# The opening of a two-layer mixer backbone in another order

## The chip, the cores and the metric

The kernel runs on one NeuronCore of a Trainium2 chip. The metric is device time in microseconds (us) for one launch. Five engines work beside each other: TensorE (PE in the profile; PEld is its weight loads), VectorE (DVE), ScalarE (ACT), GpSimd (POOL) and SyncE (SP, which here only issues transfers). Each runs its own instructions in the order in which the program gave them to it.

## The reference

Two layers over 256 latent tokens `x` and 256 context tokens `ctx`, width 1024, all in fp32.

```python
x = x + pos_embed_2d(rows)                      # before layer 0
for l in range(DEPTH):                          # DEPTH = 2
    mod = c_act @ w_mod[l] + b_mod[l]           # c_act = silu(c); ctx the same with c_ctx
    sh1, sc1, ga1, sh2, sc2, ga2 = split(mod, 6)
    h = rms_norm(x, g_norm1[l]) * (1 + sc1) + sh1
    z = h @ w_in[l]                             # 1024 x 5376
    states = s5_states(z[..., :256], discretise(lam, log_dt, b), ctx_final)
    x = x + ga1 * token_mixer(z, states, p)     # S5 readout, Fourier, pooling, convolution, gates, w_out
    x = x + ga2 * sq_relu_mlp(modulate(x, g_norm2[l], sh2, sc2), w1[l], w2[l])
return rms_norm(x, g_final)
```

`discretise` makes the recurrence's coefficients from the parameters: exponentials, a sine and a cosine, a quotient.

## The kernel before

All activations lie transposed in SBUF: `X[:, k, :]` is 128 channels by 512 tokens (context, then latent), k from 0 to 7. A product in fp32 accuracy is made of three matmuls of rounded halves: every operand is split into a high part (ScalarE, a copy into fp32r) and a low part (VectorE, a subtraction). In the profile the halves lie in tiles called `parts`, PSUM in `bank`, the recurrence's data in `scan`, X and scratch in `whole`, and most of the mixers' scratch in `mixer`. All engines' calls go through one wrapper, so that nearly every row says L64, and rows are told apart by tile and shape. Weights come as 128x1024 blocks through `Stream`: three raw slots, from which ScalarE makes the high and VectorE the low halves.

The change is in the opening, that is `run` and the first part of `layer(0)`. Its parts are these.

- **Loads.** SP's queue brings x in four blocks (`whole<-in_x_dram`), the modulation weights in 16 blocks (`in_w_mod_dram`), the first input weights (`in_w_in_dram`) and the recurrence's parameters (`in_s5p_dram`). ScalarE's queue brings the position tables, the conditioning and constants.
- **Sums of squares.** For each k the position is added to the latent half, ScalarE squares the tile, and the eight squares are added up. TensorE then sums over the partitions (four matmuls 128x1), and `norm_steps` takes the inverse root by ten small steps on VectorE. Four products of the result with the identity (`d`) and four matmuls with ones spread it to all partitions (`r`).
- **Modulation.** `parts(n)` runs n steps of `mod_part`: each is eight small matmuls (128x128 blocks, output 32x128) with one weight block. The fourth step of a set ends with a ScalarE copy of the sums (`MODSB`). `mod_finish(m)` then issues one matmul 128x8 with a selection matrix, and an addition and a scaled product on VectorE, which give shift and scale for tiles m and m+1 of h.
- **h and its products.** `next(h)` makes one tile of h: high halves on ScalarE (two ACTIVATE 128x256), the low half on VectorE and ScalarE; VectorE multiplies the next tile of X by `r`. `group(k, j)` is the product of h tile k with weight block j, three matmuls 128x512: the first needs only high halves, the second the low half of h. Four weight blocks have a PSUM bank each, into which the eight tiles of h are added. `weight(j)` has the halves of block j made.
- **Fill.** `warm(n)` issues n matmuls 128x256 whose result is not read.
- **Preparation.** `S5.prep` is a generator of small VectorE operations on 128x16 tiles (`scan<-scan`) that makes the recurrence's coefficients; `step(tab[0], n)` runs it up to its n-th next yield. When it is done, two tasks start that build tables from the coefficients, one on GpSimd and one on VectorE. They are interleaved with the mixers of layer 0 by a planner that keeps an estimated clock.

After the opening the remaining 38 blocks of the input projection, the recurrence and the other mixers follow, then projections and the MLP.

## Time and profile before

| | us |
|---|---|
| median of 3 runs | 1206.25 (1205.58 to 1209.96) |
| the profiled execution | 1209.18 |
| its span, first to last instruction | 1207.2 |
| TensorE busy | 1160.9 (96%) |
| VectorE busy | 976.1 (81%) |
| GpSimd busy | 282.9 (23%) |

The span is what the trace shows; 2 us of the profiled execution's time lie outside it. A share is an average over the span. TensorE's idle time, 46.3 us in all, lies in few places, and each of them has an engine or a transfer that it waited for.

### The profile page before, as it was taken

Reading aid. Unit: us, or ns where it says so; the run is one execution under the profiler, and the core shown is the slowest. Engines: PE = TensorE matmul, PEld = TensorE weight load, DVE = VectorE, ACT = ScalarE, POOL = GpSimd, SP = SyncE. Lnnn points to the kernel's source line nnn. Section 1 sums busy time; section 2 is a strip of 40 time slices with the busy share of each in tenths; the row PEclk is TensorE's granted clock in tenths of the full one; section 3 lists DMA queues with packets and bytes.
Section 4 is the critical chain, followed back from the end, with each engine's and each line's share of the span. In section 5 each row is a group of like instructions: output and inputs, shape, how many; then the busy total and the mean of one; then the engine's idle time right before and its main releaser. Section 6 shows DMA issues by size and latency. Waiting matters only on the chain.

```text
span 1207.2 us, 20297 instructions
## 1 busy us (share of the span) xinstructions
PE 1160.9 (96%) x7770; PEld 1009.4 (84%) x7770; DVE 976.1 (81%) x1878; ACT 517.1 (43%) x872; POOL 282.9 (23%) x319
## 2 busy tenths in 40 slices
PE   7999897999999999999999899999899999999997
PEld 5777675777888988888887778898899999999997
DVE  6789989977999769999988883546998788867764
ACT  4534242344324365422332333346544556645543
POOL 0038656000000100166555561020520001000000
PEclk9999999999999999999999999999899999999999
DMA  9543531644674514466578774425554545555551
GB/s 366 225 144 109 180 92 52 229 156 138 212 229 156 173 37 148 140 188 230 186 245 296 249 247 180 130 98 177 173 166 167 159 160 205 177 190 179 189 182 48
DMA packets 66513, 211.49 MB, mean 175 GB/s; under 512 B 7984, under 2 KB 13616, under 8 KB 66416
## 3 DMA queue, kind: packets, MB, share of 16 engines
q1 hardware_dynamic: 55456, 183.84, 45.4%
q10 hardware_dynamic: 7696, 14.56, 3.3%
q0 software_dynamic: 3264, 11.80, 2.9%
q8 instruction: 61, 1.00, 0.3%
q14 instruction: 36, 0.29, 0.1%
HBM read 199.19 MB, written 10.98 MB: 174 GB/s over the span
## 4 chain that ended last, share of the span: by engine, by line
PE 72%; DVE 15%; POOL 3%; DMA 3%; issue 3%; ACT 3%; ACTq 0%; POOLq 0%; DVEq 0%; SPq 0%
PE bank L64 72%; DVE scan L64 5%; DVE parts L64 4%; DVE mixer L64 2%; DVE whole L64 2%; ACT parts L64 2%; POOL tables L64 1%; POOL whole L64 1%; ACT whole L64 1%; DVE windows L64 1%; POOL scan L64 1%; DMA whole<-in_w_in_dram 1%; DMA whole<-in_x_dram 0%; DMA scan<-scr_z 0%; DMA scr_c<-tables 0%
## 5 line engine op out<-in xcount | busy, mean ns | idle before, releaser
L64 PE MATMUL bank<-parts 128*128 128x512 f32 (+2 forms) x4008 | 727.2, 339 | 19.0 <-DVE parts L64 16.6
L64 PEld LDWEIGHTS bank<-parts 128*128 128x128 f32 x4008 | 616.3, 191 | 105.4 <-DVE parts L64 22.3
L64 ACT ACTIVATE parts<-whole 128x1024 fp32r<-128x1024 f32 (+1 forms) x288 | 273.7, 959 | 144.9 <-PE bank L64 73.9
L64 DVE TENSOR_TENSOR parts<-whole,parts 128x1024 fp32r<-128x1024 f32 (+1 forms) x240 | 294.0, 1233 | 16.0 <-ACT parts L64 15.6
L64 PE MATMUL bank<-hidden,parts 128*128 128x256 f32 (+1 forms) x1440 | 251.2, 335 | 0.0
L64 PEld LDWEIGHTS bank<-hidden,parts 128*128 128x128 f32 x1440 | 217.5, 188 | 29.9 <-issue 0.3
L64 DVE SCALAR_TENSOR_TENSOR whole<-whole 128x1024 f32<-128x1024 f32 (+4 forms) x188 | 175.7, 936 | 15.2 <-DMA whole<-in_w_modt_dram 12.0
L64 POOL TENSOR_TENSOR whole<-whole 128x256 f32<-128x256 f32 (+1 forms) x69 | 50.3, 743 | 347.2 <-ACT whole L64 342.2
L64 DVE SCALAR_TENSOR_TENSOR whole<-bank,whole 128x256 f32<-128x256 f32 (+1 forms) x121 | 54.7, 475 | 66.4 <-PE bank L64 66.2
L64 ACT ACTIVATE whole<-whole 128x256 f32<-128x256 f32 (+2 forms) x139 | 48.9, 388 | 107.2 <-DVE whole L64 96.4
L64 ACT ACTIVATE mixer<-bank 128x512 f32<-128x512 f32 (+1 forms) x84 | 40.7, 496 | 119.8 <-PE bank L64 110.3
L64 DVE TENSOR_TENSOR whole<-whole 128x256 f32<-128x256 f32 (+7 forms) x158 | 73.0, 467 | 16.7 <-ACT whole L64 11.7
L64 ACT ACTIVATE whole<-bank 128x512 f32<-128x512 f32 (+2 forms) x69 | 35.5, 537 | 109.1 <-PE bank L64 77.5
L64 POOL TENSOR_TENSOR tables<-tables,whole 128x256 f32<-128x256 f32 x48 | 61.4, 1287 | 37.4 <-DMA scr_c<-tables 34.9
L64 DVE TENSOR_TENSOR hidden<-whole,hidden 128x512 fp32r<-128x512 f32 (+2 forms) x77 | 53.4, 698 | 9.0 <-ACT hidden L64 2.4
L64 ACT ACTIVATE hidden<-whole 128x512 fp32r<-128x512 f32 (+2 forms) x77 | 47.1, 615 | 8.2 <-PE bank L64 2.3
L64 ACT ACTIVATE tables<-bank 128x512 f32<-128x512 f32 (+2 forms) x20 | 8.4, 422 | 92.8 <-PE bank L64 92.5
L64 POOL COPY whole<-whole 128x32 f32<-128x32 f32 x20 | 11.9, 626 | 150.3 <-DVE whole L64 150.3
L64 POOL TENSOR_TENSOR scan<-scan,whole 128x256 f32<-128x256 f32 (+3 forms) x50 | 44.0, 892 | 12.0 <-DVE scan L64 8.3
L64 DVE SCALAR_TENSOR_TENSOR scan<-scan,whole 128x512 f32<-128x512 f32 (+1 forms) x64 | 42.7, 728 | 0.0
L64 PE MATMUL bank<-merged,parts 128*128 128x256 f32 (+1 forms) x240 | 38.0, 316 | 0.8 <-DVE merged L64 0.8
L64 DVE TENSOR_TENSOR scan<-scan,whole 128x256 f32<-128x256 f32 (+5 forms) x61 | 31.5, 543 | 9.0 <-ACT whole L64 8.0
(115 smaller groups left out, 899.0 us busy)
## 6 DMA issues: line engine op xcount, KB each, us to landing
whole<-in_w_dram SPq DMA_DIRECT2D x128, 512.0 KB, 4.3
whole<-in_w_in_dram SPq DMA_DIRECT2D x84, 512.0 KB, 4.3
whole<-in_w_modt_dram SPq DMA_DIRECT2D x78, 512.0 KB, 4.1
whole<-in_w_br_dram SPq DMA_DIRECT2D x16, 512.0 KB, 4.4
whole<-in_w_out_dram SPq DMA_DIRECT2D x16, 512.0 KB, 4.2
mixer<-in_w_mod_dram SPq DMA_DIRECT2D x8, 512.0 KB, 9.7
scan<-scr_b POOLq DMA_DIRECT2D x8, 512.0 KB, 5.2
scan<-in_w_mod_dram SPq DMA_DIRECT2D x6, 512.0 KB, 9.7
```

Of the source, the lines that this page charges most:

```text
L64: return f(out, *a, **k)
```

## The change

The parameters' first 48 columns are loaded ahead of x, and `prep` is stepped from the start: a `yield` is added between its two loads, and 17 of its steps lie in the opening, where it was 10. The two position loads become one, issued first. All position additions run on VectorE, where GpSimd had three of the eight. Squares are added in pairs (four additions in place of seven), and TensorE sums each pair over the partitions as it comes, into one bank, four matmuls a pair. The fill matmuls ahead of this are 3, with 1 after each of the first two pairs, where it was 7. Loads of modulation and input weights alternate in another order, and the modulation steps and products of h are interleaved one by one. `d` is made ahead of `mod_finish(0)`.

```diff
         K.nc.sync.dma_start(par, K.I["s5p"][self.l][:, 0:48])
+        yield
         K.nc.sync.dma_start(raw, K.I["s5p"][self.l][:, 48:560])
...
-    def norm_steps(self, accs, n, width, d=None):
+    def norm_steps(self, accs, n, width, d=None, pss=None):
-        pss = [self.aux() for _ in accs]
+        pss = pss or [self.aux() for _ in accs]
...
 
+            prep = tab[0]
             parts(2)
-            self.warm(2)
-            norm = self.norm_steps(((self.ACC,),), 512, 1024)
+            norm = self.norm_steps((), 512, 1024, pss=[self.sums])
             next(norm)
             self.warm(2)
             parts(1)
-            self.warm(0)
+            self.warm(1)
+            y = [y for y in norm][-1]
             parts(1)
-            y = [y for y in norm][-1]
-            self.warm(1)
+            d = self.tmp()
+            for i in range(4):
+                nc.vector.tensor_scalar(d[:, 128 * i:128 * i + 128], self.ident, y[:, i:i + 1], None, op0=MUL)
             self.mod_finish(0)
-            self.warm(2)
-            d, r = self.tmp(), self.aux()
+            r = self.aux()
             for i in range(4):
                 sl = slice(128 * i, 128 * i + 128)
-                nc.vector.tensor_scalar(d[:, sl], self.ident, y[:, i:i + 1], None, op0=MUL)
                 nc.tensor.matmul(r[:, sl], self.ones, d[:, sl], start=True, stop=True)
-            self.warm(4)
+            self.warm(2)
             h = self.h_tiles(l, 0, r, 0, 512)
+            next(h)
             weight(0)
             next(h)
+            group(0, 0)
             next(h)
-            group(0, 0)
-            self.stream.advance(1)
+            self.step(prep, 1)
             self.mod_ahead = 16
             parts(1)
-            next(h)
+            group(1, 0)
+            parts(1)
             weight(1)
+            self.step(prep, 2)
+            group(0, 1)
             parts(1)
-            group(1, 0)
-            weight(2)
-            parts(2)
-            group(0, 1)
+            group(1, 1)
+            parts(1)
             self.mod_finish(2)
             next(h)
             next(h)
-            group(1, 1)
+            self.step(prep, 1)
+            group(2, 0, 1)
+            parts(1)
+            weight(2)
+            group(3, 0, 1)
+            parts(1)
+            self.step(prep, 3)
             group(0, 2)
             group(1, 2)
-            self.step(tab[0], 3)
-            group(2, 0, 1, 2)
             parts(1)
+            group(2, 2)
             weight(3)
-            group(3, 0)
             parts(1)
-            group(3, 1)
-            parts(1)
-            parts(1)
-            group(3, 2)
             self.mod_finish(4)
             next(h)
             next(h)
+            self.step(prep, 1)
+            group(3, 2)
             group(0, 3)
             group(1, 3)
+            parts(1)
+            group(4, 0, 1, 2)
+            parts(1)
+            group(5, 0, 1, 2)
+            parts(1)
             group(2, 3)
             group(3, 3)
-            self.step(tab[0], 3)
-            group(4, 0, 1)
-            parts(2)
-            group(4, 2)
-            parts(2)
-            group(4, 3)
+            parts(1)
             self.mod_finish(6)
+            self.step(prep, 2)
             next(h)
             next(h)
-            self.step(tab[0], 3)
-            group(5, 0, 1, 2, 3)
+            group(4, 3)
+            group(5, 3)
+            self.step(prep, 2)
             group(6, 0, 1, 2, 3)
             group(7, 0, 1, 2, 3)
         else:
...
-        prow, pcol = self.SCRA(16), self.SCRA(256)
+        pos = self.SCRA(272)
+        nc.scalar.dma_start(pos, I["pos"])
-        nc.scalar.dma_start(prow, I["pos"][:, 0:16])
-        nc.scalar.dma_start(pcol, I["pos"][:, 16:272])
-        for k in range(0, 8, 2):
-            nc.sync.dma_start(self.X[:, k:k + 2, :], I["x"][:, k:k + 2, :])
...
 
         self.tab0.append(self.start(make0(), "d", 0.0))
-        self.mod_load()
-        while self.stream.load():
-            pass
-        self.step(self.tab0[0], 1)
-        self.mod_ahead = 8
+        prep = self.tab0[0]
+        self.step(prep, 1)
+        for k in range(0, 8, 2):
+            nc.sync.dma_start(self.X[:, k:k + 2, :], I["x"][:, k:k + 2, :])
+        for ahead in (3, 4, 8):
+            self.mod_ahead = ahead
+            self.mod_load()
+            self.stream.load()
+            if ahead == 4:
+                self.step(prep, 1)
+        self.mod_ahead = 10
         self.mod_load()
         nc.vector.memset(self.CACT, 0.0)
-        self.warm(7)
+        self.step(prep, 2)
         t = self.tmp()
         nc.scalar.activation(t[:, 0:16], cc, AF.Sigmoid)
         nc.vector.tensor_tensor(self.CACT[:, :, 0:2], t[:, 0:16].rearrange("p (k c) -> p k c", c=2),
                                 cc.rearrange("p (k c) -> p k c", c=2), op=MUL)
-        pr = prow.rearrange("p (k r) -> p k r", k=4)
-        pc = pcol.rearrange("p (k r) -> p k r", k=4)
+        pr = pos[:, 0:16].rearrange("p (k r) -> p k r", k=4)
+        pc = pos[:, 16:272].rearrange("p (k r) -> p k r", k=4)
+        self.warm(3)
+        self.sums = self.aux()
         sq = []
         for k in range(8):
             x = self.X[:, k, 256:512].rearrange("p (r c) -> p r c", r=4)
             pe = bc(pr[:, k, :, None], [128, 4, 64]) if k < 4 else bc(pc[:, k - 4, None, :], [128, 4, 64])
-            (nc.gpsimd if k in (1, 3, 5) else nc.vector).tensor_tensor(x, x, pe, op=ADD)
+            nc.vector.tensor_tensor(x, x, pe, op=ADD)
             sq.append(self.ACC if k == 0 else self.SIGR[k % 4] if k < 5 else self.TMP[k % 4])
             nc.scalar.activation(sq[k], self.X[:, k, :], AF.Square)
-            if k in (3, 4):
-                nc.vector.tensor_tensor(sq[k - 3], sq[k - 3], sq[k - 1], op=ADD)
-        V = nc.vector.tensor_tensor
-        for i, j in ((1, 5), (0, 4), (0, 1), (0, 6), (0, 7)):
-            V(sq[i], sq[i], sq[j], op=ADD)
+            if k % 2:
+                nc.vector.tensor_tensor(sq[k - 1], sq[k - 1], sq[k], op=ADD)
+                for i in range(4):
+                    nc.tensor.matmul(self.sums[:, i:i + 1], sq[k - 1][:, 128 * i:128 * i + 128], self.ones[:, 0:1],
+                                     start=k == 1 and i == 0, stop=k == 7 and i == 3)
+                if k < 5:
+                    self.warm(1)
+        self.step(prep, 1)
```

The first place is the start of TensorE's program, up to the spreading of the norm. `bank_63` with 128x256 is fill, 128x1 are sums of squares, 32x128 are modulation steps. Before:

```order
L64 MATMUL bank_63<-whole 128x256 x7
L64 MATMUL bank_70<-whole 32x128 x8
L64 MATMUL bank_70<-mixer,whole 32x128 x8
L64 MATMUL bank_63<-whole 128x256 x2
L64 MATMUL bank_68<-whole 128x1 x4
L64 MATMUL bank_63<-whole 128x256 x2
L64 MATMUL bank_70<-mixer,whole 32x128 x16
L64 MATMUL bank_63<-whole 128x256
L64 MATMUL bank_69<-whole 128x8
L64 MATMUL bank_63<-whole 128x256 x2
L64 MATMUL bank_67<-whole 128x128 x4
L64 MATMUL bank_63<-whole 128x256 x4
```

And now:

```order
L64 MATMUL bank_63<-whole 128x256 x3
L64 MATMUL bank_68<-whole 128x1 x4
L64 MATMUL bank_63<-whole 128x256
L64 MATMUL bank_68<-whole,mixer 128x1 x4
L64 MATMUL bank_63<-whole 128x256
L64 MATMUL bank_68<-whole,mixer 128x1 x4
L64 MATMUL bank_68<-whole 128x1 x4
L64 MATMUL bank_70<-whole 32x128 x8
L64 MATMUL bank_70<-mixer,whole 32x128 x8
L64 MATMUL bank_63<-whole 128x256 x2
L64 MATMUL bank_70<-mixer,whole 32x128 x8
L64 MATMUL bank_63<-whole 128x256
```

The sums stand ahead of all modulation steps, in four sets, and the fill ahead of them has become shorter.

The second place is TensorE around `mod_finish(2)`, whose matmul is `bank_68<-whole 128x8`; `parts` 128x512 are products of h. Before, from the first product's end:

```order
L64 MATMUL bank_70<-mixer,whole 32x128 x8
L64 MATMUL bank_70<-scan,whole 32x128 x8
L64 MATMUL bank_64<-parts 128x512 x3
L64 MATMUL bank_70<-scan,whole 32x128 x16
L64 MATMUL bank_65<-parts 128x512 x3
L64 MATMUL bank_68<-whole 128x8
L64 MATMUL bank_65<-parts 128x512 x3
L64 MATMUL bank_66<-parts 128x512 x6
L64 MATMUL bank_64<-parts 128x512 x3
L64 MATMUL bank_65<-parts 128x512 x3
L64 MATMUL bank_66<-parts 128x512 x3
```

And now, from the sixth modulation step:

```order
L64 MATMUL bank_70<-scan,whole 32x128 x8
L64 MATMUL bank_65<-parts 128x512 x3
L64 MATMUL bank_70<-scan,whole 32x128 x8
L64 MATMUL bank_65<-parts 128x512 x3
L64 MATMUL bank_70<-scan,whole 32x128 x8
L64 MATMUL bank_68<-whole 128x8
L64 MATMUL bank_64<-parts 128x512 x3
L64 MATMUL bank_65<-parts 128x512 x3
L64 MATMUL bank_70<-scan,whole 32x128 x8
L64 MATMUL bank_64<-parts 128x512 x3
```

Before, nine matmuls of h tiles 0 and 1 stand between that matmul and the first of tile 2. Now the last modulation step stands directly ahead of it, and products of tile 2 directly behind it.

The third place is VectorE around `mod_finish(6)`, whose two operations are `128x2x4` and `128x4`; `scan` 128x16 is preparation, `parts` rows are low halves of h and weights. Before, the finish is followed by h tile 6:

```order
L64 TENSOR_TENSOR whole<-bank_68,whole 128x2x4
L64 SCALAR_TENSOR_TENSOR whole<-whole 128x4
L64 TENSOR_SCALAR whole<-whole 128x256
L64 TENSOR_TENSOR whole<-whole,bank_67 128x512
L64 TENSOR_TENSOR parts<-whole,parts 128x256
L64 SCALAR_TENSOR_TENSOR parts<-whole 128x256
L64 TENSOR_SCALAR whole<-whole 128x256
L64 TENSOR_TENSOR parts<-whole,parts 128x256
L64 SCALAR_TENSOR_TENSOR parts<-whole 128x256
```

And now:

```order
L64 TENSOR_TENSOR whole<-bank_68,whole 128x2x4
L64 SCALAR_TENSOR_TENSOR whole<-whole 128x4
L64 TENSOR_SCALAR scan<-scan 128x16 x2
L64 SCALAR_TENSOR_TENSOR scan<-scan 128x16
L64 TENSOR_TENSOR scan<-scan 128x16 x2
L64 TENSOR_SCALAR scan<-scan 128x16 x2
L64 SCALAR_TENSOR_TENSOR scan<-scan 128x16
L64 TENSOR_SCALAR whole<-whole 128x256
L64 TENSOR_TENSOR whole<-whole,bank_67 128x512
L64 TENSOR_TENSOR parts<-whole,parts 128x256
L64 SCALAR_TENSOR_TENSOR parts<-whole 128x256
L64 TENSOR_SCALAR whole<-whole 128x256
```

Eight preparation operations have come between the finish and h tile 6.

## Rows read from the trace of the kernel before

**Rows 1.** Head of the page: span, and TensorE's busy time.
```profile
span 1207.2 us, 20297 instructions
...
PE 1160.9 (96%) x7770; PEld 1009.4 (84%) x7770; DVE 976.1 (81%) x1878; ACT 517.1 (43%) x872; POOL 282.9 (23%) x319
```
**Rows 2.** Waits of TensorE over the whole span: total, times, longest.
```profile
PE bank L64 <- DVE parts L64: 16.6, 10, 7.8
...
PE bank L64 <- POOL scan L64: 3.9, 2, 2.1
```
**Rows 3.** Windows by stage: length, each engine's busy time, granted clock, DMA share, GB/s.
```profile
77.40:211.40 134.00, 118.33 (x707) 92.06 (x705) 126.94 (x219) 48.23 (x121) 92.27 (x112) 0.95 0.32 107
211.40:427.00 215.60, 214.95 (x1304) 176.00 (x1304) 182.81 (x302) 80.17 (x113) 9.43 (x12) 0.99 0.54 181
```
**Rows 4.** Timeline of TensorE in the opening: start, time, instructions, idle before.
```profile
4.47 6.32 PE L64 MATMUL bank<-whole 128*128 128x256 f32 x14 [4.47 <-DMA whole<-in_x_dram]
...
17.59 4.44 PE L64 MATMUL bank<-whole 128*128 128x256 f32 x24
22.54 0.50 PE L64 MATMUL bank<-parts 128*128 128x512 f32 x1 [0.51 <-ACT parts L64]
23.60 0.73 PE L64 MATMUL bank<-parts 128*128 128x512 f32 x2 [0.56 <-DVE parts L64]
...
26.07 0.73 PE L64 MATMUL bank<-parts 128*128 128x512 f32 x2 [0.29 <-DVE parts L64]
26.74 1.08 PE L64 MATMUL bank<-scan,whole 128*32 128x128 f32 x32
...
28.55 0.28 PE L64 MATMUL bank<-whole 128*128 128x8 f32 x2
28.69 2.52 PE L64 MATMUL bank<-parts 128*128 128x512 f32 x10
31.48 2.11 PE L64 MATMUL bank<-parts 128*128 128x512 f32 x8 [0.27 <-DVE parts L64]
...
46.57 9.77 PE L64 MATMUL bank<-parts 128*128 128x512 f32 x42
```
**Rows 5.** Timeline of VectorE in the opening.
```profile
13.08 1.49 DVE L64 TENSOR_TENSOR whole<-whole 128x512 f32<-128x512 f32 x2
15.71 0.16 DVE L64 TENSOR_SCALAR whole<-bank 128x4 f32<-128x4 f32 x1 [1.15 <-PE bank L64]
...
19.54 1.22 DVE L64 TENSOR_TENSOR parts<-whole,parts 128x1024 fp32r<-128x1024 f32 x1
...
28.87 0.17 DVE L64 TENSOR_TENSOR whole<-bank,whole 128x8 f32<-128x8 f32 x1 [0.58 <-PE bank L64]
...
30.94 0.48 DVE L64 SCALAR_TENSOR_TENSOR parts<-whole 128x256 fp32r<-128x256 f32 x1 [0.32 <-ACT whole L64]
...
42.74 0.80 DVE L64 SCALAR_TENSOR_TENSOR scan<-scan 128x16 f32<-128x16 f32 x4
```
**Rows 6.** Timeline of ScalarE in the opening.
```profile
27.88 0.28 ACT L64 ACTIVATE whole<-bank 128x128 f32<-128x128 f32 x1 [1.44 <-PE bank L64]
29.27 1.09 ACT L64 ACTIVATE parts<-whole 128x256 fp32r<-128x256 f32 x2 [1.11 <-DVE whole L64]
```
**Rows 7.** Window of TensorE with two lone modulation steps among h products.
```profile
33.52:36.47 2.95, 2.95 (x39) 1.72 (x39) 2.15 (x7) 0.00 (x0) 0.00 (x0) 1.00 1.02 408
```
**Rows 8.** Window that starts with TensorE's pause at 92.
```profile
92.00:95.90 3.90, 3.87 (x13) 2.93 (x14) 3.83 (x6) 1.98 (x6) 3.82 (x5) 0.57 0.17 67
```
**Rows 9.** Timeline of TensorE after the opening, two pauses.
```profile
92.03 0.39 PE L64 MATMUL bank<-scan 128*32 128x112 f32 x4 [2.05 <-POOL scan L64]
...
211.41 17.58 PE L64 MATMUL bank<-parts 128*128 128x512 f32 x68 [7.84 <-DVE parts L64]
```
**Rows 10.** Timeline of VectorE in layer 0's mixers.
```profile
158.69 1.22 DVE L64 TENSOR_TENSOR parts<-whole,parts 128x1024 fp32r<-128x1024 f32 x1 [4.75 <-ACT parts L64]
...
210.67 1.29 DVE L64 TENSOR_TENSOR parts<-mixer,parts 128x512 fp32r<-128x512 f32 x2
```

## The prediction

> **What bounds the kernel now.** I read the head of the page first: TensorE is busy 1160.9 of 1207.2 us [rows 1]. No matmul of the computation is removed, so time can come only out of TensorE's 46.3 us of idling or out of the clock, and can go only into new idling. The list of TensorE's waits says where the idling is: 16.6 us behind VectorE's halves in ten waits, one of them 7.8, and 3.9 behind GpSimd's recurrence work in two [rows 2]. By place, the windows say that between 77 and 211 us, the mixers of layer 0, TensorE is busy 118.33 of 134.00 and VectorE 126.94: here VectorE sets the end. From 211 to 427 TensorE is busy 214.95 of 215.60, so whatever is late or early there is swallowed [rows 3]. The change lies ahead of both, in the first 55 us. I read that stretch row by row, because the planner's later work is displaced as a whole by however much the opening ends later or earlier.
>
> In the opening, TensorE waits until the first two halves of h tile 0 are there: the first product starts at 22.54, its second matmul at 23.60, behind VectorE's low half [rows 4]. I call the start of that second matmul M. From M on TensorE is nearly dense: the two pauses that remain are 0.29 and 0.27. The last 42 rows run in 9.77, 0.233 a matmul, so the 36 of them that belong to the opening end at 46.57 + 36 x 0.233 = 55.0 [rows 4]. M to the end takes 31.4 us. Since the same modulation steps (12) and products (31 and two thirds of 32) stand behind M before and after, the change can gain in the opening only by bringing M forward, and every new wait behind M is lost.
>
> **The change, part by part.**
>
> *Up to M.* Before, the last addition of squares ends at 14.57 (13.08 + 1.49), and the norm starts at 15.71 [rows 5]. The new order makes a chain of each pair on two engines: two position additions, two squares, an addition, and the next pair's additions queue behind that on VectorE. An addition 128x512 is 0.75 [rows 5]; with a square and two position additions of a few tenths each, estimated from it by size, a pair takes about 2.3, four take 9.2, and from a start at 5 to 6 the last ends at 14.4 to 15.4. So fewer additions do not come out earlier. TensorE's sums follow, 0.8 later, and then four modulation steps, which used to stand partly ahead of the sums and now all stand behind; the fourth ends near 18.7, the finish gives the scale at 19.7, and the first scaled tile, 0.68, is followed on VectorE by the low half of weight block 0 (1.22 [rows 5]) and the rest of h tile 0. That puts M at about 24.0, 0.4 later. Bounds: 22.0 if the pairs and the steps overlap better and the weight half is not in the way, 25.5 with the later start. What lies beside it: the moved preparation steps cost VectorE 0.2 an operation (0.80 for four [rows 5]), in stretches where it waits for x or TensorE.
>
> *Finish 2.* Measured before, with its matmul at 28.55: VectorE's operations at 28.87, ScalarE's high halves at 29.27 for 1.09, VectorE's low half at 30.94, and TensorE's second matmul of h tile 2 at 31.48, which is 2.93 behind the selection matmul [rows 4 to 6]. Nine matmuls of earlier tiles (of the ten in 2.52) covered that but for 0.27. The selection itself comes about 1.0 after the start of the last modulation step: 0.6 for the step, and the copy of 0.28 [rows 6] with the handing over. Now the last step stands directly ahead and h tile 2 directly behind. The second matmul then starts 3.9 after the step's start, where a covered one would start about 0.9 after it: **+3.0**. The pause has the form 0.4, then about 1.7, one matmul, then 0.8.
>
> *Finish 4.* Behind it stand nine matmuls (tiles 3, 0 and 1) and a step, 2.7 us, so that only the wait for the copy shows: **+0.4**.
>
> *Finish 6.* Six matmuls stand behind it, 1.4 us, against the 1.85 after which the high half is there: 0.4 for the copy and 0.3 for that. VectorE has eight preparation operations between the finish and h tile 6: 8 x 0.2 = 1.5 with overlap, on the path of the low half, and there is nothing left to fill: second matmul 1.9 later. Together **+2.6**. The high half does not wait for VectorE's preparation, and h tile 7 is covered by tile 6's 12 matmuls.
>
> *Interleaving one by one.* Two lone modulation steps and six matmuls take 2.95 [rows 7]; bare, that is 2 x 0.5 (two in a row: 1.08 [rows 4]) + 6 x 0.233 = 2.4. So a lone step costs about 0.25 more than one of a pair. Before, 12 steps stand in 7 places, now in 12: **+1.3**.
>
> *Less the pauses of before:* 0.29 + 0.27 = **-0.56**. M to end: 3.0 + 0.4 + 2.6 + 1.3 - 0.6 = +6.7, which is 38.1 us.
>
> *The clock.* After the pause of 2.05 at 92.03 the granted clock reads 0.57 for the next 3.9 us: the lower of the two levels, 1.2 of 2.4 GHz, for most of them [rows 8, 9]. At half speed a stretch of 3.4 us does 1.7 us of work. Finish 2 and finish 6 make pauses of about that length. I take one such loss, **+1.7**, and none or two for the range.
>
> *The mixers.* Preparation ends some 14 us earlier against the end of the opening, and both table tasks start with it. But between the first gate and the last low half that TensorE waits for, VectorE has nearly the same work; by the order of its instructions it has about 2.6 us less, while a heap of preparation and table work right behind the opening delays the first gate by 1.3. GpSimd's tables reach TensorE's first products earlier, which can save a short wait of 0.6. **-1.9**. VectorE's long idle time there, 4.75 at 158.69 behind ScalarE [rows 10], stays in this sum: bound -6.6 if it goes as well, and +3 if the heap keeps the gate back further. The stall at 211.41 of 7.84, whose releasing low half starts at 210.67 straight behind the recurrence [rows 9, 10], moves with it.
>
> Sum: 0.4 + 6.7 + 1.7 - 1.9 = **+6.9**. The trace's execution took 1209.18, of which 1207.2 is span; it lies 2.9 above the median, and I put the sum on the median: 1206.25 + 6.9 = 1213.2.
>
> **Rivals.**
>
> *No change within 0.5% (6.0 us, about what a measurement of this kernel tells from none).* For it: M could come at 22.0 (-2.0 against the sum), the pauses may not lower the clock (-1.7), and some of the 4.75 may go, since GpSimd's chain, on which ScalarE waited there, starts earlier (-2). That gives 1206.25 + 6.9 - 5.7 = 1207.5. Against: finish 2, finish 6 and the switches are in program order and do not depend on these.
>
> *Faster.* The tables come early enough that VectorE no longer idles between 77 and 211: 4.75 and 0.6, with GpSimd's waits of TensorE (3.9 [rows 2]) and the slow clock behind them (2 x 1.7) gone, and the stall of 7.84 shrinking with VectorE's earlier end. It is decided by whether VectorE is idle between the first gate and the low half at 210.67; if not at all, that end comes 6.6 + 3.4 = 10 us earlier, and with the last slow stretch after the stall gone, and M at 22, the sum is +6.9 - 2 - 8.1 - 5 = -8.2: 1198. Against: VectorE is busy 95% of that stretch [rows 3], and its work there is not moved by the change.
>
> *A colder start.* The first seven fill matmuls ran in 6.32 us, 0.45 a row; the row of 24 from 17.59 on took 4.44, under 0.2 each [rows 4]. So TensorE begins at the lower level and has the higher one by then. Only three fill matmuls stand in a row now, then single ones among short sums. If the lower level lasts until the products of h are under way, the norm's spreading and the first 4 us or so of products run at half speed: +4 on the sum, 1217.2. The Trainium skill ("TensorE: Matmul & The Clock Gate", Part 1: The HAM clock gate) says that the throttled level is the default and that activity releases it; the rows of the first fill agree, and by that rule the shortened fill speaks for this rival. No run here shows yet how little of it is enough.
>
> **How the numbers follow.** Chances: the sum as it stands 0.35, the colder start 0.23, no change 0.30, faster 0.12. The likeliest gives 1213.2. The sum with its bounds (M, one slow stretch more or less, the gate) runs from 1208 to 1218, the cold start on to 1221; downwards I go to 1202.5, which leaves out most of the faster case and little above. Of the sum's own chance a small part falls below 1212.3, the bound for slower, as does little of the cold start; some of the no-change case lies beyond it. Faster 0.12, same 0.33, slower 0.55.
>
> **What would show it.** In the changed kernel's trace: the second matmul of the first product near 24; behind the second 128x8 matmul two pauses with one matmul between, together near 2.5 us, released by ScalarE's and VectorE's halves; behind the fourth one a pause near 2 before the second matmul of h tile 6, with VectorE in `scan` 128x16 operations; and the last product of the opening near 62. The granted clock in the first 30 us tells the cold start. In the mixers, VectorE's idle time ahead of the low half of the first branch and TensorE's wait for it. I am wrong if M comes before 21.5, if the finishes' chains take less than 2 us, or if TensorE's stall of 7.8 is gone.

## The result, and the profile after

The changed kernel is slower: 1217.44 us at the median of eight runs, against 1206.88 for the kernel before, ratio 1.0075 (95% interval 1.0050 to 1.0101), which is +9.1 us by the ratio (the two medians lie 10.6 apart). The profiled execution took 1215.86, with a span 6.9 us longer than before's [rows 1]. The head of its page, and TensorE's busy time:

```profile
span 1214.1 us, 20291 instructions
...
PE 1163.2 (96%) x7778; PEld 1007.2 (83%) x7778; DVE 972.7 (80%) x1878; ACT 518.4 (43%) x872; POOL 276.4 (23%) x316
```

TensorE is again busy for 96%. Its timeline up to the first products of h (answers to [rows 4]; columns as there):

```profile
5.49 2.93 PE L64 MATMUL bank<-whole 128*128 128x256 f32 x6 [5.49 <-DMA whole<-in_x_dram]
...
13.05 1.20 PE L64 MATMUL bank<-whole 128*128 128x256 f32 x2
...
15.61 2.85 PE L64 MATMUL bank<-whole 128*128 128x1 f32 x24
18.24 1.08 PE L64 MATMUL bank<-mixer,whole 128*32 128x128 f32 x16
19.25 2.01 PE L64 MATMUL bank<-whole 128*128 128x256 f32 x4
...
21.76 0.70 PE L64 MATMUL bank<-whole 128*128 128x256 f32 x2
22.39 0.64 PE L64 MATMUL bank<-mixer,whole 128*32 128x128 f32 x16
23.43 2.25 PE L64 MATMUL bank<-whole 128*128 128x8 f32 x14 [0.40 <-ACT whole L64]
26.72 0.50 PE L64 MATMUL bank<-parts 128*128 128x512 f32 x1 [1.04 <-ACT parts L64]
28.38 0.73 PE L64 MATMUL bank<-parts 128*128 128x512 f32 x2 [1.16 <-DVE parts L64]
```

The second matmul of the first product, M in the prediction, starts at 28.38; before it was 23.60. The last pair's sums begin at 15.61, and behind them stand step 0 (the end of that row), step 1 (18.24), two fills (19.25), step 2, a fill (21.76), step 3 (22.39) and the finish's matmul (23.43). The pitch of the fill tells the clock: two rows in 1.20 at 13.05, four in 2.01 at 19.25, two in 0.70 at 21.76. Up to about 21 TensorE ran at the lower level. (The clock column of a window reads 1.00 there, as it does from 0 to 21 in this trace; it does not show this slow start.) VectorE there (answers to [rows 5]):

```profile
14.63 0.69 DVE L64 TENSOR_TENSOR whole<-whole 128x512 f32<-128x512 f32 x1 [0.88 <-ACT whole L64]
...
17.49 0.16 DVE L64 TENSOR_SCALAR whole<-bank 128x4 f32<-128x4 f32 x1 [1.67 <-PE bank L64]
...
23.86 0.17 DVE L64 TENSOR_TENSOR whole<-bank,whole 128x8 f32<-128x8 f32 x1 [3.12 <-PE bank L64]
...
24.85 0.69 DVE L64 TENSOR_TENSOR whole<-whole,bank 128x512 f32<-128x512 f32 x1 [0.63 <-PE bank L64]
25.46 1.22 DVE L64 TENSOR_TENSOR parts<-whole,parts 128x1024 fp32r<-128x1024 f32 x1
...
27.85 0.48 DVE L64 SCALAR_TENSOR_TENSOR parts<-whole 128x256 fp32r<-128x256 f32 x1
```

The last addition of squares ends at 15.32, and the norm starts at 17.49, 2.2 later (before: 1.1 [rows 5]). The finish finds VectorE waiting for 3.12, and behind the first scaled tile (24.85) it makes the low half of the weights (25.46) before the low half of h tile 0 (27.85): TensorE's 1.16 ahead of M. From there to the end of the opening:

```profile
33.77 0.64 PE L64 MATMUL bank<-scan,whole 128*32 128x128 f32 x16
34.81 0.39 PE L64 MATMUL bank<-whole 128*128 128x8 f32 x2 [0.40 <-ACT whole L64]
36.78 0.49 PE L64 MATMUL bank<-parts 128*128 128x512 f32 x1 [1.58 <-ACT parts L64]
37.84 2.27 PE L64 MATMUL bank<-parts 128*128 128x512 f32 x5 [0.56 <-DVE parts L64]
...
47.51 0.39 PE L64 MATMUL bank<-whole 128*128 128x8 f32 x2 [0.40 <-ACT whole L64]
...
58.92 0.39 PE L64 MATMUL bank<-whole 128*128 128x8 f32 x2 [0.40 <-ACT whole L64]
59.16 2.22 PE L64 MATMUL bank<-parts 128*128 128x512 f32 x7
62.84 7.33 PE L64 MATMUL bank<-parts 128*128 128x512 f32 x31 [1.45 <-DVE parts L64]
```

At the second finish (34.81) the pauses are 0.40, 1.58 and 0.56 with one matmul between; the two later ones show 0.40 each, and the last also 1.45 ahead of the second matmul of h tile 6. The 23 matmuls of the opening that are left at 62.84 end at 62.84 + 23 x 0.2325 = 68.2, where before they ended at 55.0. Two windows (columns as in [rows 3]):

```profile
38.00:41.40 3.40, 3.40 (x22) 2.07 (x23) 3.30 (x11) 2.66 (x4) 0.00 (x0) 0.52 0.06 22
91.80:217.80 126.00, 114.89 (x707) 88.44 (x705) 122.25 (x206) 46.79 (x117) 80.70 (x99) 0.99 0.32 108
```

Behind the second finish the granted clock was 0.52: the lower of the two levels, 1.2 of 2.4 GHz. And the stretch of the mixers, from VectorE's first gate to the last low half that TensorE waits for, is 126.0 long, where it was 134.0 [rows 3]. TensorE at its end (answers to [rows 9]), and ScalarE:

```profile
217.88 13.09 PE L64 MATMUL bank<-parts 128*128 128x512 f32 x47 [4.64 <-DVE parts L64]
232.77 1.75 PE L64 MATMUL bank<-scan 128*32 128x128 f32 x80 [1.79 <-ACT scan L64]
```

```profile
230.74 1.97 ACT L64 ACTIVATE scan<-windows 128x1024 f32<-128x1024 f32 x1 [1.17 <-DMA windows<-scr_k]
```

The pause that was 7.84 is 4.64. But 15 us later TensorE waits 1.79 for ScalarE, and ScalarE for a transfer of windows, where the kernel before waited 0 to 0.4.

### The profile page after: what moved, and what is told of

The parts are those of the page before. It is cut to its first block, busy times and chain, and to the rows that moved or that the text cites. A ratio compares the mean times of both kernels' runs of the same rounds, so it can differ in the third digit from the quotient of the medians.

```text
span 1214.1 us, 20291 instructions
## 1 busy us (share of the span) xinstructions
PE 1163.2 (96%) x7778; PEld 1007.2 (83%) x7778; DVE 972.7 (80%) x1878; ACT 518.4 (43%) x872; POOL 276.4 (23%) x316
## 4 chain that ended last, share of the span: by engine, by line
PE 70%; DVE 12%; DMA 7%; POOL 4%; issue 3%; ACT 2%; ACTq 0%; SPq 0%; DVEq 0%; POOLq 0%
PE bank L64 70%; DVE scan L64 4%; DVE parts L64 4%; DMA whole<-in_w_in_dram 3%; POOL tables L64 2%; DMA scr_c<-tables 2%; DVE mixer L64 2%; POOL whole L64 2%; DVE whole L64 2%; ACT parts L64 1%; ACT whole L64 1%; DVE windows L64 1%; DMA whole<-in_const_dram 1%; DMA scan<-scr_b 1%; DMA windows<-scr_k 0%
## 5 line engine op out<-in xcount | busy, mean ns | idle before, releaser
L64 PEld LDWEIGHTS bank<-parts 128*128 128x128 f32 x4008 | 611.5, 190 | 109.8 <-DVE parts L64 24.4
L64 DVE SCALAR_TENSOR_TENSOR whole<-whole 128x1024 f32<-128x1024 f32 (+3 forms) x186 | 173.6, 934 | 23.4 <-DMA whole<-in_w_modt_dram 16.7
L64 POOL TENSOR_TENSOR whole<-whole 128x256 f32<-128x256 f32 (+1 forms) x69 | 54.6, 805 | 357.8 <-ACT whole L64 352.0
L64 POOL TENSOR_TENSOR tables<-tables,whole 128x256 f32<-128x256 f32 x48 | 57.0, 1194 | 40.6 <-DMA scr_c<-tables 32.7
L64 DVE TENSOR_TENSOR scan<-scan,whole 128x256 f32<-128x256 f32 (+5 forms) x61 | 31.4, 541 | 16.7 <-ACT whole L64 13.6
L64 DVE TENSOR_TENSOR mixer<-mixer 128x512 f32<-128x512 f32 (+11 forms) x60 | 35.8, 602 | 6.0 <-ACT mixer L64 5.3
```

The lines of the kernel that those rows point to most:

```text
L64: return f(out, *a, **k)
```

## Experiments

All kernels give the same four marks. M is the start of the second matmul of the first product; E the end of the opening, worked out as above from the row that holds its last products (in early and cover2 the granted clock fell within that row, and E is the start of the first product behind the opening's: 70.49 and 68.41); Y the row where TensorE resumes behind the low half of the first branch (211.41 before, 217.88 after). The ratio is against runs of the kernel before on the same chip. Marks come from the one profiled execution of each, ratios from all its runs.

| kernel | M | M to E | E to Y | Y to the span's end | ratio to before (95%) |
|---|---|---|---|---|---|
| before | 23.60 | 31.3 | 156.5 | 995.8 | |
| before_again | 23.81 | 31.3 | 156.5 | 991.4 | |
| before_again2 | 24.44 | 31.3 | 156.4 | 992.9 | |
| changed | 28.38 | 39.8 | 149.7 | 996.2 | 1.0075 (1.0050 to 1.0101) |
| after_again | 28.84 | 40.7 | 149.9 | 997.3 | |
| before_prep | 28.42 | 31.4 | 149.9 | 997.8 | 1.0004 (0.9986 to 1.0022) |
| fill10_only | 24.10 | 31.3 | 154.0 | 995.3 | 0.9980 (0.9960 to 1.0001) |
| before_fill | 23.86 | 31.3 | 150.1 | 994.5 | 0.9968 (0.9950 to 0.9987) |
| fill7 | 28.34 | 39.8 | 149.6 | 992.0 | 1.0059 (1.0038 to 1.0081) |
| early | 27.75 | 42.7 | 148.2 | 995.7 | 1.0072 (1.0050 to 1.0094) |
| dense | 27.17 | 38.3 | 149.3 | 994.2 | 1.0045 (1.0025 to 1.0064) |
| cover2 | 30.37 | 38.0 | 148.7 | 1004.6 | 1.0051 (1.0032 to 1.0070) |
| prep6 | 28.88 | 39.0 | 150.1 | 993.9 | 1.0066 (1.0042 to 1.0091) |
| fixed | 26.33 | 34.4 | 150.5 | 992.2 | 1.0012 (0.9988 to 1.0035) |

Theory after the result: early preparation shortens the mixers; the opening gives it back and more, by a late M and by what it puts behind M. Rivals: the mixers' gain is a by-product of the late opening; M is late by clock alone, or by order alone.

**before_prep: the early preparation alone.** The loads and steps of the change, in the opening of before (shown in part; the last edit stands in three places):

```diff
+        prep = self.tab0[0]
+        self.step(prep, 1)
         for k in range(0, 8, 2):
             nc.sync.dma_start(self.X[:, k:k + 2, :], I["x"][:, k:k + 2, :])
...
+        self.step(prep, 2)
...
-            self.step(tab[0], 3)
+            self.step(tab[0], 4)
```

> The kernel before, with only the early recurrence parameters and 17 preparation steps in its own opening (steps at the same early places, later ones by four in place of three). Theory: the 6.7 us that the changed kernel regains between the end of the opening and VectorE's low half of the first branch come from the early preparation alone. Then the second matmul of the first product stays at 23.6 (+-0.5), the opening ends at 55 to 55.5, and that stretch is 149 to 151 us where it was 156.4; time 6 us shorter than before, near 1200.5. Rival: the regain is a by-product of the late opening (loads and halves get ahead while VectorE idles 19 us in it); then the stretch stays at 155 to 157 and the time at 1206 to 1207.

E to Y came to 149.9 with the opening of before. But M stood at 28.42 in this execution, as late as in the changed kernel, so that the rival falls only with before_fill below; and the median, forecast near 1200.5, gained nothing. Windows and TensorE's timeline ahead of M:

```profile
10.40:13.60 3.20, 1.23 (x23) 0.59 (x25) 3.17 (x6) 1.96 (x4) 0.15 (x1) 1.00 1.01 412
13.80:23.80 10.00, 10.00 (x70) 7.68 (x62) 4.35 (x21) 1.22 (x2) 0.00 (x0) 0.50 1.03 417
```

```profile
12.35 0.64 PE L64 MATMUL bank<-whole 128*32 128x128 f32 x16 [1.46 <-DMA whole<-in_w_mod_dram]
13.51 0.99 PE L64 MATMUL bank<-mixer,whole 128*32 128x128 f32 x16 [0.51 <-DMA mixer<-in_w_mod_dram]
14.43 5.49 PE L64 MATMUL bank<-whole 128*128 128x256 f32 x16
...
28.42 0.73 PE L64 MATMUL bank<-parts 128*128 128x512 f32 x2 [0.57 <-DVE parts L64]
```

The granted clock was 1.00 from 10.4 to 13.6 and 0.50 from 13.8 to 23.8. Ahead of the fall TensorE had waited 1.46 and 0.51 for modulation weights. The same fill and sums as in before then took 5.49 where they had taken 3.26.

**before_again, before_again2: before, unedited, twice more.**

> The kernel before, unchanged, in another execution. If the start of the second matmul at 23.6 belongs to this kernel, it stands at 23.3 to 24.0 here; if the granted clock's rise differs from execution to execution, it may stand anywhere up to 28.5, with everything between it and 158 us later by the same amount.

> The same once more: 23.3 to 24.0 if that start belongs to the kernel, up to 28.5 if it differs from execution to execution.

M at 23.81 and 24.44: within 0.9 us. The stretches up to Y repeat to 0.1; Y to the end differs by 4.4 between executions.

**after_again: the changed kernel, unedited, once more.**

> The changed kernel, unchanged, in another execution: second matmul of the first product at 28.4 (+-0.7) if its late start belongs to the kernel, at 25.5 or earlier if the profiled execution was unlucky.

28.84. Its late M belongs to it; cover2 and prep6, which do not differ from the changed kernel up to M, have 30.37 and 28.88. M to E is 0.9 longer than in the first execution: the granted clock was 0.50 from 29 to 32 as well.

**fill7: seven fills again.**

```diff
-        self.warm(3)
+        self.warm(7)
```

> The changed kernel with seven fill matmuls ahead of the sums in place of three. Theory: the lower granted clock up to about 21 us makes most of the 4.8 us by which the second matmul of the first product is later (28.38 against 23.60): it comes to 25 to 26, and the time falls by 2.5 to 3. Rival: the order is the cause (all four modulation steps and their fill stand behind the last sums); then it stays at 28 to 28.5, or later, since the fill at the lower clock takes 6.3 us and pushes the sums back.

The rival held: M 28.34. But the windows show that this does not acquit the clock:

```profile
10.50:13.70 3.20, 3.20 (x25) 2.93 (x23) 2.31 (x6) 1.15 (x2) 0.00 (x0) 1.00 1.02 419
13.90:20.50 6.60, 5.81 (x49) 5.05 (x50) 3.78 (x20) 1.07 (x2) 0.00 (x0) 0.51 1.03 419
```

The higher level was there at 10.5, and went again from 13.9 to 20.5, while TensorE did sums and steps with single fills.

**early: steps and weight halves ahead, fill between the steps out.**

```diff
+                if k == 5:
+                    self.mod_part()
+                    self.mod_part()
...
-            parts(2)
             norm = self.norm_steps((), 512, 1024, pss=[self.sums])
             next(norm)
-            self.warm(2)
             parts(1)
-            self.warm(1)
             y = [y for y in norm][-1]
+            self.stream.high()
             parts(1)
...
+            weight(0)
             self.mod_finish(0)
...
             next(h)
-            weight(0)
             next(h)
```

> The changed kernel with modulation steps 0 and 1 ahead of the last pair's sums, no fill between steps 2 and 3, and the halves of weight block 0 made ahead of the first finish. Theory: its late first product comes from the order on TensorE (the seven fills left it at 28.3) and from the weight half on VectorE between the first scaled tile and h tile 0. Then the first finish's matmul comes at 20 to 20.5 in place of 23.4, and the second matmul of the first product at 24 to 25.5 in place of 28.4; time 3 to 4 us below the changed kernel. Rival: with the fill gone TensorE stays at the lower clock longer, the norm's spreading and the first products run at half speed, and the opening ends within 1.5 us of the changed kernel's.

The theory fell. TensorE, ahead of M and at the end of the opening, VectorE at the norm's start, and the window ahead of M:

```profile
18.08 1.87 PE L64 MATMUL bank<-whole 128*128 128x1 f32 x8
...
22.21 4.28 PE L64 MATMUL bank<-whole 128*128 128x8 f32 x14 [0.40 <-ACT whole L64]
...
63.51 7.14 PE L64 MATMUL bank<-parts 128*128 128x512 f32 x23 [1.46 <-DVE parts L64]
```

```profile
19.98 0.16 DVE L64 TENSOR_SCALAR whole<-bank 128x4 f32<-128x4 f32 x1 [2.87 <-PE bank L64]
```

```profile
12.80:26.30 13.50, 13.10 (x100) 10.68 (x100) 8.15 (x29) 4.08 (x8) 0.00 (x0) 0.50 1.03 417
```

The weight half is out of the way (M follows the first matmul by 1.06, not 1.66), but the finish comes at 22.21 only, and the spreading of the norm behind it takes 4.28, where it took 2.25 in the changed kernel: at a granted clock of 0.50 throughout. VectorE no longer waits for the finish, and M stands 7.8 behind the norm's start (19.98), as in before (7.9). But that start has moved from 17.49 to 19.98: steps 0 and 1 now stand ahead of the last sums (18.08), all of it at the lower level. M, 27.75, gained 0.6 and the time nothing. The clock also fell to 0.50 at 36.8 to 43.5 and at 64.1 to 67.4, so that M to E is 2.9 longer than in the changed kernel (the last 23 products, from 63.51, took about 7).

**dense: that order, with fill everywhere.** Against early:

```diff
-        self.warm(3)
+        self.warm(7)
...
-                if k < 5:
-                    self.warm(1)
+                if k < 7:
+                    self.warm(2)
                 if k == 5:
                     self.mod_part()
                     self.mod_part()
+                    self.warm(2)
```

(and two fills, one, two and four at the places where before had them, up to the spreading)

> The changed kernel with the order of steps and halves of the earlier try (steps 0 and 1 ahead of the last sums, weight block 0 ahead of the finish), and with fill wherever TensorE would wait: seven at the start, two after each pair's sums, and between and behind the steps as the kernel before had it. Theory: the late first product is the lower clock and the order together, neither alone. Then the granted clock rises near 10 and stays, the second matmul of the first product comes at 24 to 25 in place of 28.4, from there to the end of the opening it is 39.8 as in the changed kernel, and the time is 3.5 to 4.5 us below the changed one. Rival: the fill delays the sums and steps by what the clock gains, and the second matmul stays at 27 or later.

By M the rival held, 27.17; by the ratios the time is 3.6 us below the changed kernel's, as the theory had it. From 11 on the clock stays at the higher level, but the seven fills, the first sums and two fills more last until 13.2, and the later sums and steps queue behind them, step 0 at 17.1 and steps 2 and 3 at 20.5 (before: 11.68 and 16.58):

```profile
5.47 7.73 PE L64 MATMUL bank<-whole 128*128 128x256 f32 x26 [5.47 <-DMA whole<-in_x_dram]
...
17.66 2.89 PE L64 MATMUL bank<-whole 128*128 128x256 f32 x16
...
27.17 0.73 PE L64 MATMUL bank<-parts 128*128 128x512 f32 x2 [0.57 <-DVE parts L64]
```

```profile
19.61 0.16 DVE L64 TENSOR_SCALAR whole<-bank 128x4 f32<-128x4 f32 x1 [3.12 <-PE bank L64]
```

The last addition of squares ends at 15.98, but the norm starts only at 19.61: steps 0 and 1 and their fill stand ahead of the last sums. M follows the norm by 7.6. So the order takes away the wait of 3.1 for the finish, and starts the norm 2.1 later than in the changed kernel.

A second finding lies further on. The pauses of the second finish are those of the changed kernel, and the clock did not fall behind them:

```profile
35.55 0.51 PE L64 MATMUL bank<-parts 128*128 128x512 f32 x1 [1.58 <-ACT parts L64]
36.62 1.43 PE L64 MATMUL bank<-parts 128*128 128x512 f32 x5 [0.56 <-DVE parts L64]
```

Five matmuls take 1.43, where they took 2.27. M to E is 38.3 in place of 39.8: 1.5 is what that one fall cost.

**cover2: nine matmuls behind the second finish.**

```diff
             group(0, 1)
+            weight(2)
-            parts(1)
-            group(1, 1)
-            parts(1)
+            parts(2)
             self.mod_finish(2)
             next(h)
             next(h)
             self.step(prep, 1)
-            group(2, 0, 1)
+            group(1, 1)
+            group(0, 2)
+            group(1, 2)
+            group(2, 0, 1, 2)
             parts(1)
-            weight(2)
             group(3, 0, 1)
             parts(1)
             self.step(prep, 3)
-            group(0, 2)
-            group(1, 2)
             parts(1)
-            group(2, 2)
```

> The changed kernel with nine matmuls of h tiles 0 and 1 behind the second finish's matmul again, as before, weight block 2 made ahead of it, and modulation steps 6 and 7 in a row. Theory: the two pauses there (1.58 and 0.56) go but for some 0.3, and with them the slow clock behind them (1.7): from the second matmul of the first product to the end of the opening 35.5 to 36.5 us in place of 39.8; time 3.5 to 4 us below the changed kernel. Rival: the pauses only move to weight block 2 or to the next finish, and the stretch stays over 38.5.

The pauses went as forecast, to 0.40 and 0.26. M to E is 38.0, 1.8 less than in the changed kernel and not the 3.3 to 4.3 of the theory: this execution had falls of the clock elsewhere, at 31.2 to 34.6 and among the last 23 products, which took about 7 in place of 5.3. fixed, below, has the same edit without any fall.

```profile
36.95 0.39 PE L64 MATMUL bank<-whole 128*128 128x8 f32 x2 [0.40 <-ACT whole L64]
37.19 2.54 PE L64 MATMUL bank<-parts 128*128 128x512 f32 x10
39.98 2.10 PE L64 MATMUL bank<-parts 128*128 128x512 f32 x8 [0.26 <-DVE parts L64]
...
61.44 7.13 PE L64 MATMUL bank<-parts 128*128 128x512 f32 x23 [1.46 <-DVE parts L64]
```

```profile
61.90:65.30 3.40, 3.40 (x10) 2.65 (x9) 2.27 (x13) 1.48 (x2) 0.00 (x0) 0.50 0.69 234
```

The median gained 2.9 by the ratios (1.0075 - 1.0051), inside the intervals of both; this profiled execution itself was one of the slowest, with M at 30.37 and 1004.6 behind Y.

**prep6: the preparation behind h tiles 6 and 7.**

```diff
             self.mod_finish(6)
-            self.step(prep, 2)
             next(h)
             next(h)
+            self.step(prep, 2)
```

> The changed kernel with the two preparation steps behind the fourth finish moved behind h tiles 6 and 7. Theory: the pause of 1.45 ahead of the second matmul of h tile 6 goes, the opening ends 1.4 earlier, and the time falls by 1 to 1.5. Rival: the preparation is what the mixers wait for, so that what the opening gains comes back as a stretch 1.5 longer up to the first branch's low half, and the time stays.

```profile
62.49 7.78 PE L64 MATMUL bank<-parts 128*128 128x512 f32 x33 [0.56 <-DVE parts L64]
```

The pause is 0.56 in place of 1.45, M to E 39.0: 0.9 gained, not 1.4, since the low half of tile 6 still comes later than the products ahead of it last. E to Y is 0.4 longer. Of the total the ratio shows 0.0009, too little for its interval.

**fixed: dense, cover2 and prep6 together.** No further edit.

> The dense kernel with the nine covering matmuls behind the second finish and the preparation behind h tiles 6 and 7 as well. If the three causes found make up the whole loss: second matmul at 24 to 25, from there to the end 35.5, on to the first branch's low half 150, so that this comes at 210 and the time is 7 to 8 us below the changed kernel, within 2 us of before. Rival: something else of the change costs time, and it stays 4 us or more above before.

1.0012 of before (0.9988 to 1.0035), and 7.6 us below the changed kernel by the ratios. That makes up nearly the whole loss against before, but not what the new opening costs: before_fill below has the same preparation in the old opening and stands at 0.9968, some 5 us lower. The marks say where they are: M is 2.5 later than there and M to E 3.1 longer, which the mixers' gain of 6 hides against before. Against dense, which has no fall of the clock behind M either, M to E is 3.9 shorter; 0.9 of that is prep6's, and the other 3.0 is what cover2's edit (nine covering matmuls, steps 6 and 7 in a row) is worth where the clock does not fall.

```profile
34.77 2.11 PE L64 MATMUL bank<-parts 128*128 128x512 f32 x8 [0.25 <-DVE parts L64]
```

**fill10_only and before_fill: ten fills in before, without and with early preparation.**

```diff
-        self.warm(7)
+        self.warm(10)
```

> The kernel before with ten fill matmuls in place of seven and no early preparation. If the gain of the kernel with both (0.9968 of before) is the early preparation's, this one stays within 1 us of before, with 156.5 from the end of the opening to the first branch's low half. Rival: the gain is the fill's, by a steadier clock at the start: then this one gains 3 us or more too.

> The kernel before with early preparation and ten fill matmuls at the start in place of seven. Theory: the early preparation alone shortens the mixers by 6.4 us, but its profiled execution lost 4.8 of it since the granted clock fell again at 13.7, after the waits for the first modulation weights. With three more fills TensorE has no such waits; the second matmul of the first product comes at 23.6 to 24.5, and the time is 3 to 6 us below before. Rival: the clock's start is a matter of the single execution and not of three fills; then the median stays within 2 us of before.

before_fill is faster than both kernels: 0.9968 of before (0.9950 to 0.9987), 3.9 us. M is at 23.86, with the clock at the higher level all the way:

```profile
5.18 7.39 PE L64 MATMUL bank<-whole 128*128 128x256 f32 x36 [5.18 <-DMA whole<-in_x_dram]
...
23.86 0.73 PE L64 MATMUL bank<-parts 128*128 128x512 f32 x2 [0.56 <-DVE parts L64]
```

```profile
9.80:24.00 14.20, 12.53 (x117) 9.31 (x116) 12.05 (x36) 5.63 (x10) 0.28 (x1) 1.00 1.03 417
```

fill10_only stands at 0.9980, 2.4 us, between theory and rival, its interval just touching 1. So how much of the 3.9 is fill and how much preparation is not settled by the times. By the marks, E to Y is 150.1 with preparation, with M on time: the mixers' gain does not come from a late opening. Without preparation it is 154.0 to 156.5 (the 154.0 has 1.26 of VectorE's idle time where before had 4.75). So 3.9 of the gain is shown for the preparation, with the same fill; the other 2.5 came once without it. In that execution the clock stayed at the higher level from 77.9 to 204.2, where before had 0.50 at 92.6 to 95.9, 130.2 to 133.4 and 160.9 to 164.2. What made that difference was not tried.

## Why the prediction came out

The time was forecast at 1213.2, +6.9. The profiled execution is +6.9 by its span, the ratio says +9.1, and the median of 1217.44 lies 4.2 above the forecast, inside the range. That the sum came so near is luck: two terms were off by more than 4 us, in opposite directions.

- **M, forecast +0.4, is +4.7** (28.4 and 28.8 against 23.6 to 24.4). This is the step that failed. The chain of pairs was sized well (last addition at 15.3, forecast 14.4 to 15.4), and so was what follows the finish: its scale is there at 24.2 and M comes 4.2 later, forecast 19.7 and 4.3. Missed was TensorE in between: the fourth step, forecast to end near 18.7, ends at 23.0. The norm starts 2.2 behind the last addition, not 0.8, and all four steps, with their fill between them, stand behind the last sums, at half speed up to about 21. The colder start, held as a rival at 0.23 and +4, is what happened to the level, with the cost ahead of M and not behind it. Neither the order of early nor that order at the higher level (dense) brings M back: both take away VectorE's wait for the finish, but the norm then starts 3.4 and 3.6 behind the last addition, in early since the steps ahead of the last sums run at the lower level, in dense since fill stands there too. How much of the 4.7 is the clock and how much the order was not separated.
- **M to E, forecast 38.1 and 1.7 for the clock, is 39.8.** Second finish: 4.1 from the step's start to the second matmul (37.84 - 33.77), forecast 3.9; third 0.40 as forecast; fourth 1.85, forecast 2.6. The clock's fall behind the second finish cost 1.5 (dense). Without it 38.3, of which what is left for the lone steps is 38.3 - 31.3 + 0.6 - 3.2 - 0.4 - 1.85 = 2.1, forecast 1.3. The mechanism was right; that the sum fits to a tenth comes mainly from errors of 0.8 up and 0.75 down, which is luck again.
- **The mixers, forecast -1.9, are -6.8** (149.7 against 156.5), the stated bound being -6.6. Mis-sized, and for the reason that the bound named only in part. From the first gate to the low half the stretch is 8.0 shorter: VectorE is busy 4.7 less (122.25 in place of 126.94, where 2.6 less was forecast) and idle 3.3 less (3.75 in place of 7.06: the 4.75 [rows 10] went, a new wait of 2.17 came). The first gate came 23.7 behind E as forecast (91.88 - 68.2). before_fill shows the same with M on time, and against fill10_only 3.9 of it is the preparation's.
- **Behind Y, forecast 0, a new wait comes.** Every kernel with early preparation waits 1.4 to 3.2 there for ScalarE, behind the windows' transfer (1.17 in the row above); without it 0 to 0.4. Y to the end is 995.8 at the mean of ten such executions and 993.9 of four others, with a spread of several us in both, so that a loss in the total is not shown. What makes the transfer the last to arrive was not tried.

The rival "faster" asked that VectorE be not idle at all in the mixers. It was still idle 3.75, and what the mixers gained was lost in the opening. The prediction's reading of "under 0.2" for each of the 24 rows at 17.59 mixes fill with smaller matmuls (14 of the rows are fill); that the level was the higher one by then stands, since two fill rows take 0.70 at the one level and 1.20 at the other in the changed kernel.

## What to carry to other kernels

When an opening is reordered, write down for every wait what stood between its cause and its use, and keep that many instructions there: the edit that put nine matmuls behind a finish was worth 3 us (fixed against dense), and the one fall of the clock behind that finish cost the changed kernel 1.5 more. When work is moved ahead, ask which chain it now delays: the steps moved ahead of the last sums took away one wait and delayed the norm. Fill matmuls are part of the schedule: the thinly filled early ran at the lower level, and dense's fill ahead of a queue cost time, so the place to try them is where TensorE waits anyway. And a gain behind a bound stage (6 us in the mixers by the marks) may be had without the rearrangement in which it was delivered; of the time before_fill kept 3.9 us, fill included, and before_prep none.

## What the runs showed of the hardware

The granted clock at the start is not a property of the program alone. The opening of before kept it from 10 on in two executions and had one short fall in a third, with M within 0.9 us; the same opening with the parameters loaded first fell to half for 10 us in its profiled execution, with M 4.6 later than in before_fill. Nor is the fall behind a pause certain: the pauses of 1.58 and 0.56 were followed by it in the changed kernel (both executions), fill7, early and prep6, and not in dense; in the changed kernel it cost 1.5 us. The 29 runs of before on one chip spread from 1202.1 to 1215.7, more than the effect studied. The Trainium skill ("TensorE: Matmul & The Clock Gate", Part 1: The HAM clock gate) says that the throttled state is the default and that activity releases it; the traces agree in that the first fill runs slowly (two rows in 1.20 in the changed kernel, in 0.70 later). But the busy time in the profile does not tell the level: TensorE was busy 13.10 of 13.50 us at 0.50 in early's 12.8 to 26.3, with sums, steps and little fill, and 12.53 of 14.20 at 1.00 in before_fill's 9.8 to 24.
